# Small loads issued ahead of the opening barrier, and two split points moved, in a LoRA linear kernel

## The chip, the cores and the metric

One core of one Trainium2 chip. The time is the device time of one execution in microseconds (us), lower is better; it is quoted as the median of the runs, with lowest and highest. "Faster" and "slower" are verdicts at 2%. The span of a profile is about 1.3 us shorter than the time.

## The reference, cut to what matters

```python
x = randn(16, 2048, 256)            # fp32; W 256x256, A 256x16, B 16x256, E 16, scale 1.0
x_flat = x.reshape(-1, in_dim)      # 32768 x 256
y = x_flat @ W
lora_out = ((x_flat @ lora_A) * lora_E) @ lora_B
y = y + scale * lora_out            # 32768 x 256, fp32
```

33.6 MB are read and 33.6 MB are written, for one small matrix product. The kernel folds A, E and B into one matrix, weff = W + A diag(E) B, once at its start.

## The kernel before: the parts that the change and the argument touch

The 32768 rows are 4 chunks of 64 rows per partition (8.4 MB each). The kernel keeps three chunks at a time in SBUF, the on-chip memory, in three "homes"; chunk 3 uses the home of chunk 0 again, so its loads wait until the rows of chunk 0 that they overwrite have been stored. Results are written over x in its home. All loads and stores of rows are issued by one engine, SP, in the order of one list:

```python
ORDER = [
    ("L", 0, 0, 8),          # load, chunk, first row, end row
    ("W",),
    ("L", 0, 8, 24), ("L", 0, 24, 40), ("L", 0, 40, 64),
    ("L", 1, 0, 32), ("L", 1, 32, 64),
    ("L", 2, 0, 16), ("L", 2, 16, 64),
    ("S", 0, 0, 44),         # store
    ("S", 0, 44, 64),
    ("L", 3, 0, 44),
    ("L", 3, 44, 64),
    ("S", 1, 0, 64), ("S", 2, 0, 64), ("S", 3, 0, 64),
]
HELD = (2, 16)                   # from this row on the cast waits for the store in HOLDERS
HOLDERS = (("S", 0, 0, 44),)
...
    def sync_program():
        for n, op in enumerate(ORDER):
            ...
            if kind == "L":
                for st in stored:            # stores of the rows that this load overwrites
                    if st[1] == c - N_HOMES and st[2] < e and s < st[3]:
                        sync.wait_ge(stored[st], 16)
                ins = sync.dma_start(out=at_home, in_=x_chunks[c, :, s:e, :]).then_inc(loaded[op], 16)
                if n == 0:
                    opening.append(ins.ins.name)     # issued ahead of the opening barrier
            else:
                sync.wait_ge(s_done, ends.index((c * ROWS + e) // CG - 1) + 1)
                sync.dma_start(out=y_chunks[c, :, s:e, :], in_=at_home).then_inc(...)
```

A group of 4 rows passes through four engines: POOL casts it to bf16 (line 176 of this kernel), PE transposes it (226), DVE copies the transpose to SBUF (210), PE multiplies by weff (237), ACT copies the result into the home (193). The setup needs A, E, B and W, in this order. Everything named in `opening` is moved ahead of the barrier that all engines pass at the start; before the change, these are the first rows of x and A. The final wait of SP for the last stores is line 268. PE is the matrix engine; DVE, ACT and POOL are the vector, scalar and general-purpose engines; SP issues transfers. The 16 DMA engines, which move the data, are meant where the text below speaks of "the engines" of a queue or of "one engine" that is slow.

## Time and profile before

161.79 us when the prediction was made (median of 3, 161.79 to 162.03).

| what | value | where read |
|---|---|---|
| span | 160.5 us | page |
| main DMA queue, share of 16 engines | 98.3% | page, part 3 |
| bytes over the span | 420 GB/s | page, part 3 |
| busiest compute engine (PE) | 61% | page, part 1 |
| end of compute of chunk 3 | 121.97 us | timeline of ACT |
| SP waits for the last stores | 36.7 us | waits of SP |

These lines are from the page of the kernel before: span; PE, POOL, granted clock of PE (PEclk, tenths of full speed) and DMA share in 40 slices of 4 us (the other digits are tenths of busy time); the main queue with packets, MB, share; the bytes.

```profile
span 160.5 us, 2023 instructions
...
PE   5999999959999991000899948999991000000000
...
POOL 1526758477777740001677716777720000000000
PEclk9999999999999999755599995999999555555555
DMA  7999999999999998999999899997997997997991
...
q1 hardware_dynamic: 2304, 67.37, 98.3%
...
HBM read 33.85 MB, written 33.55 MB: 420 GB/s over the span
...
```

DMA is at 9 in nearly every slice (the 7s and 8s further on come from long packets that are counted where they start; in the packet records no engine idles there), while PE and POOL have a long hole (slices 15 to 18, counted from 0, where the cast of chunk 2 is held) and nothing at all in the last quarter.

The chain of waits of the kernel before seems to say something else. The columns are start, duration in us, and what:

```profile
...
2.48 20.82 DMA home<-in_x_dram
...
28.46 47.02 DMA out_dram<-home
...
75.50 20.25 DMA home<-in_x_dram
...
120.96 1.01 ACT home L193
```

The store issued at 28.46 us takes 47.02 us "to land", and the chain then follows compute of chunk 3. But this is a place in a queue, not a slow store: all loads of chunks 0 to 2 are ahead of it. The view of SP's timeline (start, time over which the group is issued, instruction) shows how early the issues are, and the waits of SP (total us, times, longest) show how long SP waits for the last stores when all is issued:

```profile
...
0.00 0.38 SPq L147 DMA_DIRECT2D home<-in_x_dram  x1
1.14 0.33 SPq L139 DMA_DIRECT2D w_sb<-in_W_dram  x1
1.52 3.54 SPq L147 DMA_DIRECT2D home<-in_x_dram  x7
28.46 8.76 SPq L152 DMA_DIRECT2D out_dram<-home  x2
75.50 7.19 SPq L147 DMA_DIRECT2D home<-in_x_dram  x2
82.73 39.63 SPq L152 DMA_DIRECT2D out_dram<-home  x3
```

```profile
...
SPq L268 <- SPq L268: 36.7, 1, 36.7
...
```

Seven loads of x, 24 MB, are in the queue by 5.1 us. The start of the kernel before, in the timeline of all engines:

```profile
...
1.10 0.38 ACTq L187 DMA_DIRECT2D e_sb<-in_lora_E_dram  x1
...
1.15 0.20 POOL L155 MEMSET ident<- 128x128 f32 x1 [0.71 <-SPq L272]
1.51 0.45 ACTq L187 DMA_DIRECT2D b_sb<-in_lora_B_dram  x1
...
7.47 2.07 PE L259 MATMUL psum_y<-b_sb,ate 16*128 16x256 f32 x4 [0.30 <-DMA b_sb<-in_lora_B_dram]
...
9.64 0.69 DVE L214 TENSOR_TENSOR weff<-w_sb,psum_y 128x512 bf16<-128x512 f32 x1 [1.75 <-PE psum_y L259]
...
```

The barrier is passed at about 1.1 us; the identity is made (1.15), E and B are issued (1.10, 1.51), the product with B runs at 7.47 and weff is made at 9.64 us.

Beside these views the argument uses the trace's records of single DMA packets (start, duration, bytes), which no view prints; tables of them stand in plain fences. One packet is one partition's share of a load or store, so 8 packets per engine and transfer. At full rate a 64 KB packet takes 2.418 us, 48 KB 1.816, 44 KB 1.665, 32 KB 1.215, 24 KB 0.912, 20 KB 0.761: 16 engines at 2.418 us per 64 KB are 433.7 GB/s.

### The profile page before, as it was taken

The numbers are of one execution on the slowest core, as the hardware profiler recorded it, in microseconds if no ns is written. First come the engines' busy times: TensorE is split into PE (matmuls) and PEld (weight loads), VectorE is DVE, ScalarE is ACT, GpSimd is POOL, SyncE is SP. The second block draws the span as 40 slices with busy tenths as digits, with TensorE's granted clock in tenths as the row PEclk, the third lists the DMA queues.
The fourth block names the chain that finished last, engine by engine and source line by source line (L and its number), as shares of the span: only waits on it lengthen the run. The fifth ranks groups of instructions, "written<-read, shape, count | busy, mean of one in ns | idle before, by whom it ended". The sixth has DMA issues, their size and how long they took to land.

```text
span 160.5 us, 2023 instructions
## 1 busy us (share of the span) xinstructions
PE 97.5 (61%) x782; PEld 84.3 (53%) x782; DVE 45.4 (28%) x66; ACT 66.1 (41%) x65; POOL 66.8 (42%) x70
## 2 busy tenths in 40 slices
PE   5999999959999991000899948999991000000000
PEld 2358988949999990000799937999990000000000
DVE  0233554525555550000255521555540000000000
ACT  3005776737777773000177751777773000000000
POOL 1526758477777740001677716777720000000000
PEclk9999999999999999755599995999999555555555
DMA  7999999999999998999999899997997997997991
GB/s 251 398 441 455 416 463 392 474 433 400 416 445 502 453 404 359 505 393 394 421 402 496 382 404 451 500 492 310 506 457 343 490 474 343 490 474 343 490 457 82
DMA packets 2515, 67.43 MB, mean 420 GB/s; under 512 B 448, under 2 KB 464, under 8 KB 592
## 3 DMA queue, kind: packets, MB, share of 16 engines
q1 hardware_dynamic: 2304, 67.37, 98.3%
q10 hardware_dynamic: 208, 0.03, 0.1%
q14 instruction: 3, 0.02, 0.0%
HBM read 33.85 MB, written 33.55 MB: 420 GB/s over the span
## 4 chain that ended last, share of the span: by engine, by line
DMA 55%; PE 17%; POOL 1%; ACT 1%; SPq 1%; issue 1%; ACTq 0%
DMA out_dram<-home 29%; DMA home<-in_x_dram 26%; PE psum_y L237 11%; PE psum_xt L226 6%; POOL stage L176 1%; ACT home L193 1%; SPq L147 1%; SPq L139 0%; ACTq L195 0%; SPq L308 0%; SPq L272 0%
## 5 line engine op out<-in xcount | busy, mean ns | idle before, releaser
L193 ACT COPY home<-psum_y 128x1024 f32<-128x1024 f32 x64 | 64.8, 1013 | 53.9 <-PE psum_y L237 53.9
L176 POOL CAST stage<-home 128x1024 bf16<-128x1024 f32 x64 | 66.1, 1040 | 49.2 <-DMA out_dram<-home 17.3
L237 PE MATMUL psum_y<-weff,xt 128*128 128x256 bf16 x512 | 69.7, 281 | 0.0
L210 DVE COPY xt<-psum_xt 128x1024 bf16<-128x1024 bf16 x64 | 44.3, 692 | 66.0 <-PE psum_xt L226 66.0
L237 PEld LDWEIGHTS psum_y<-weff,xt 128*128 128x128 bf16 x512 | 51.8, 101 | 6.5
L226 PE MATMUL psum_xt<-ident,stage 128*128 128x128 f32 x260 | 42.1, 286 | 21.2 <-POOL stage L176 21.2
L226 PEld LDWEIGHTS psum_xt<-ident,stage 128*128 128x128 f32 x260 | 32.0, 148 | 24.6 <-issue 23.4
L250 PE MATMUL psum_y<-ident 128*128 128x512 f32 x4 | 3.8, 1101 | 1.9 <-POOL ident L157 1.9
L250 PEld LDWEIGHTS psum_y<-ident 128*128 128x128 f32 x4 | 1.2, 325 | 3.0 <-POOL ident L157 1.9
L259 PE MATMUL psum_y<-b_sb,ate 16*128 16x256 f32 x4 | 2.1, 670 | 0.3 <-DMA b_sb<-in_lora_B_dram 0.3
L200 DVE TENSOR_SCALAR ate<-psum_y,e_sb 16x256 f32<-16x256 f32 x1 | 0.5, 472 | 6.3 <-PE psum_y L253 6.3
L193 ACT ACT_TABLE_LOAD x1 | 1.3, 1283 | 2.0 <-issue 2.0
L259 PEld LDWEIGHTS psum_y<-b_sb,ate 16*128 16x128 f32 x4 | 1.2, 319 | 0.9 <-DMA b_sb<-in_lora_B_dram 0.7
L214 DVE TENSOR_TENSOR weff<-w_sb,psum_y 128x512 bf16<-128x512 f32 x1 | 0.7, 689 | 1.8 <-PE psum_y L259 1.8
L253 PEld LDWEIGHTS psum_y<-ident,a_sb 128*16 128x16 f32 x2 | 0.2, 114 | 1.3 <-DMA a_sb<-in_lora_A_dram 0.9
L253 PE MATMUL psum_y<-ident,a_sb 128*16 128x128 f32 x2 | 0.6, 421 | 0.0
L155 POOL MEMSET ident<- 128x128 f32 x1 | 0.2, 204 | 0.7 <-SPq L272 0.7
L157 POOL TENSOR_SCALAR_AFFINE_SELECT ident<-ident 128x128 f32<-128x128 f32 x1 | 0.3, 292 | 0.2 <-POOL ident L155 0.2
L294 POOL MEMSET const-float32-0.0<- 128x1 f32 x1 | 0.1, 99 | 0.2 <-issue 0.2
L294 POOL MEMSET const-bfloat16-1.0<- 128x1 bf16 x1 | 0.1, 102 | 0.0
L294 POOL MEMSET const-uint8-127<- 128x1 uint8 x1 | 0.1, 102 | 0.0
L294 POOL MEMSET const-float32-1.0<- 128x1 f32 x1 | 0.1, 99 | 0.0
## 6 DMA issues: line engine op xcount, KB each, us to landing
home<-in_x_dram SPq DMA_DIRECT2D x2, 4096.0 KB, 34.7
home<-in_x_dram SPq DMA_DIRECT2D x3, 2048.0 KB, 14.0
home<-in_x_dram SPq DMA_DIRECT2D x1, 6144.0 KB, 57.6
out_dram<-home SPq DMA_DIRECT2D x1, 5632.0 KB, 47.0
home<-in_x_dram SPq DMA_DIRECT2D x1, 5632.0 KB, 20.3
home<-in_x_dram SPq DMA_DIRECT2D x1, 3072.0 KB, 20.8
out_dram<-home SPq DMA_DIRECT2D x1, 2560.0 KB, 45.5
home<-in_x_dram SPq DMA_DIRECT2D x1, 2560.0 KB, 19.5
```

The source lines that it names most:

```text
L147: ins = sync.dma_start(out=at_home, in_=x_chunks[c, :, s:e, :]).then_inc(loaded[op], 16)
L176: gpsimd.tensor_copy(out=stage[g % NS][:], in_=home(c)[:, b:b + CG, :]).then_inc(s_stage[g % UNROLL], 1)
L193: scalar.copy(out=home(c)[:, b:b + CG, :], in_=psum_y[g % NY][:]).then_inc(s_free[(g + NY) % UNROLL], 1)
L200: vector.tensor_scalar(out=ate[:], in0=psum_y[0][:R, :KT, :P], scalar1=e_sb[:], scalar2=float(scale), op0=ALU.mult, op1=ALU.mult,).then_in ...
L210: vector.tensor_copy(out=xt[g % NX][:], in_=psum_xt[g % NT][:].bitcast(BF16)).then_inc(s_xt[g % UNROLL], 1)
L214: vector.tensor_add(out=weff[:], in0=w_sb[:], in1=psum_y[1][:, :KT, :]).then_inc(s_free[0], 1)
L226: ins = tensor.transpose(psum_xt[i % NT][:, b, :], words[:, b, :], ident[:])
L237: ins = tensor.matmul(psum_y[i % NY][:, b, :], xt[i % NX][:, b, t::KT], weff[:, t, :], start=(t == 0), stop=(t == KT - 1),)
L250: tensor.matmul(psum_y[1][:, :2, :], ident[:], ident[:, None, :].to_broadcast([P, 4, P]), start=True, stop=True)
L253: ins = tensor.transpose(psum_y[0][:R, t, :P], a_sb[:, t, :], ident[:])
L259: ins = tensor.matmul(psum_y[1][:, t, :], ate[:, t, :], b_sb[:], start=True, stop=True)
L294: nc = _bacc.Bacc("TRN2", target_bir_lowering=False, num_devices=1)
```

## The change

The intent: take the setup's small loads off the path behind the barrier, so that weff is made earlier, and choose the split points so that the cast of chunk 2 and the compute of chunk 3 start earlier.

```diff
-    ("S", 0, 0, 44),
-    ("S", 0, 44, 64),
-    ("L", 3, 0, 44),
-    ("L", 3, 44, 64),
+    ("S", 0, 0, 40),
+    ("S", 0, 40, 64),
+    ("L", 3, 0, 32),
+    ("L", 3, 32, 64),
...
-HOLDERS = (("S", 0, 0, 44),)
+HOLDERS = (("S", 0, 0, 40),)
...                                    # in sync_program, the load of W
-                sync.dma_start(out=w_sb[:], in_=w).then_inc(set_up_loaded["w"], 16)
+                ins = sync.dma_start(out=w_sb[:], in_=w).then_inc(set_up_loaded["w"], 16)
+                opening.append(ins.ins.name)
...                                    # in scalar_program, the loads of A, B, E
             ("a", a_sb, lora_A.rearrange("(q t) r -> q t r", t=KT)),
+            ("b", b_sb, lora_B),
             ("e", e_sb, lora_E[:, None]),
-            ("b", b_sb, lora_B),
...
-            if name == "a":
-                opening.append(ins.ins.name)
+            opening.append(ins.ins.name)
```

The order of the instructions on each engine is otherwise the same; SP's load of W and ACT's loads of B and E move ahead of the barrier.

## The prediction

> **What bounds the kernel now.** The 16 DMA engines, from end to end. The page gives the main queue a share of 98.3% and a mean of 420 GB/s. In the trace's packet records all 16 engines are occupied from about 1.2 us (first packet 1.03) to 158.1 us of a 160.5 us span; the only holes, between 3 and 6 us, are worth 0.1 us of all engines. A 64 KB packet takes 2.418 us, so 16 engines give 433.7 GB/s. This agrees with the ceiling of 435 GB/s in the Trainium skill, "DMA: Bandwidth & Descriptors", section "Where 436 GB/s comes from". 67.37 MB at that rate are 155.3 us. The rest is 1 us of start, some 2 us of longer packets at load/store turns, and a tail: 15 engines end between 158.1 and 159.3 us, one at 160.0. That one lost 1.4 us: its 64 KB packets took 2.57 instead of 2.42 us from 100.6 to 123.7 us, while chunk 3 was computed (until 122.0).
>
> The chain of waits names a load (20.8 us), a store (47.0 us) and chunk 3's matmuls, but the queue is first-in-first-out: the store issued at 28.5 lands at 75.5 us because all earlier loads are ahead of it. Compute has slack: the stores reach chunk 3 at about 139 us, 17 us after its rows are done.
>
> **What the change does.**
> - W, A, B, E ahead of the barrier: moves four issues of 0.33 to 0.45 us. The order of the queue and the bytes stay. The first 1 MB keeps the engines busy until about 4.3 us, and the next load, issued at 1.52 us, was early enough. Three issues on ScalarE (0.12 + 0.38 + 0.45 + 0.39, ending near 1.3 us instead of 0.5) will delay the barrier by an estimated 0.4 to 0.8 us; the second load of x is issued at 1.6 to 2.0 us. Nothing starves. B lands before its wait (today 7.4 us; 0.7 us waited), but the second load of x, landing near 11 us, gates compute anyway. Worth 0 +- 0.1 us. The same page, "Issuing engines are not separate DMA queues", says that issuing elsewhere saves only sequencer time; I expect agreement.
> - Store 0 split at 40: lands about 1.2 us earlier (0.5 MB less), near 74.3 us; the held cast of chunk 2 starts then. Off the critical path.
> - Chunk 3 in halves: the first lands near 91.2 us instead of 95.8; compute ends near 116 to 118 instead of 122.0 us. Off the critical path; packets of 40, 24, 32 KB instead of 44 and 20 cost the same (estimate from the records: +0.04 us).
> - Indirect: if the one engine's slow packets come from compute beside the store of chunk 1, ending compute 5 us earlier spares it two of nine, 0.3 us of the end.
>
> **Prediction.** 161.5 us, range 160.9 to 162.1. Faster by over 2%: 0.01; within 2%: 0.98; slower: 0.01.
>
> **What would show it.** Loads of x up to chunk 2 and the last three stores land within 0.2 and 0.5 us of before; mean 419 to 422 GB/s; in the timeline W is issued before 1 us, the second load of x at 1.6 to 2.0; the first store within 1 us of 28.5; compute of chunk 3 ends 4 to 6 us earlier without moving the end.
>
> **What would make it wrong.** A hole in the queue: a chunk-3 load issued after the queue drained (today 6 to 7 us of remaining store cover it); a barrier so late that engines idle at 4 us; or another engine lagging, up to 1 us either way.

## The result, and the profile after

| kernel | median us | lowest to highest | runs | ratio to before, 95% interval |
|---|---|---|---|---|
| before | 161.71 | 161.61 to 162.03 | 6 | |
| after | 161.59 | 161.40 to 161.92 | 6 | 0.9993 (0.9976 to 1.0009) |
| after, repeated in later rounds | 161.32 | 161.20 to 162.46 | 6 | 0.9990 (0.9960 to 1.0020) |

If there is a gain, it is 0.1%, and neither interval excludes none. The same lines of the page after:

```profile
span 160.4 us, 2024 instructions
...
PE   2969978959999991000899999999930000000000
...
POOL 1527838477777740001657777787300000000000
PEclk9999999999999999655579999999995555555555
DMA  7999999999999997989999999997998998998992
...
q1 hardware_dynamic: 2304, 67.37, 98.5%
...
HBM read 33.85 MB, written 33.55 MB: 420 GB/s over the span
...
```

The DMA row is again at 7 to 9 in every slice but the last, and the 420 GB/s are the same; PE and POOL end a slice earlier (the last PE digit that is not 0 moves from slice 30 to 29). Chain, timeline of SP, wait for the last stores, and start:

```profile
...
2.95 20.34 DMA home<-in_x_dram
...
27.14 48.41 DMA out_dram<-home
...
75.66 1.05 POOL stage L177
...
```

```profile
...
0.43 0.42 SPq L139 DMA_DIRECT2D w_sb<-in_W_dram  x1
2.10 3.39 SPq L148 DMA_DIRECT2D home<-in_x_dram  x7
27.14 10.06 SPq L153 DMA_DIRECT2D out_dram<-home  x2
75.56 7.74 SPq L148 DMA_DIRECT2D home<-in_x_dram  x2
83.35 35.85 SPq L153 DMA_DIRECT2D out_dram<-home  x3
```

```profile
...
SPq L268 <- SPq L268: 39.7, 1, 39.7
...
```

```profile
...
0.55 0.45 ACTq L188 DMA_DIRECT2D b_sb<-in_lora_B_dram  x1
1.02 0.44 ACTq L188 DMA_DIRECT2D e_sb<-in_lora_E_dram  x1
...
2.10 0.20 POOL L156 MEMSET ident<- 128x128 f32 x1 [1.66 <-SPq L272]
...
7.83 1.10 PE L259 MATMUL psum_y<-b_sb,ate 16*128 16x256 f32 x4
...
9.03 0.69 DVE L214 TENSOR_TENSOR weff<-w_sb,psum_y 128x512 bf16<-128x512 f32 x1 [0.58 <-PE psum_y L259]
...
```

Everything that the change meant to move has moved. W is issued at 0.43 instead of 1.14 us, B at 0.55 instead of 1.51, weff is made at 9.03 instead of 9.64, store 0 is issued at 27.14 instead of 28.46, compute of chunk 3 ends at 118.80 instead of 121.97 (timeline of ACT). And there is a price: the barrier is passed 0.95 us later (the identity at 2.10 instead of 1.15), because ACT issues until 1.46 us. The chain of waits has another shape (it now goes through the cast of chunk 2 at 75.66), yet the time is the same. Of the 3.2 us that compute gained, 3.0 reappear in one place: SP's wait for the last stores grew from 36.7 to 39.7 us.

One more thing changed. POOL's timeline, first of the kernel before, then of the one after, and the last result of chunk 3 in the one after:

```profile
...
95.81 2.02 POOL L176 CAST stage<-home 128x1024 bf16<-128x1024 f32 x2 [4.16 <-DMA home<-in_x_dram]
...
```

```profile
...
93.44 1.04 POOL L177 CAST stage<-home 128x1024 bf16<-128x1024 f32 x1 [0.34 <-PE psum_xt L226]
...
117.79 1.01 ACT L193 COPY home<-psum_y 128x1024 f32<-128x1024 f32 x1 [0.30 <-PE psum_y L237]
...
```

Before the change, the cast of chunk 3 waits 4.16 us for the first part of its load. After it, POOL waits for no load of chunk 3: from the held cast at 75.66 us on, it waits for PE alone. So the end of compute is now set by when that cast starts and by the pace of compute, not by the load of chunk 3.

The landings, first to last of the 16 engines, from the trace's landing records (us from the start of the span):

```
transfer              before             after              after, repeated
load 2, rows 16-64    61.61 to 62.16     61.95 to 63.37     61.72 to 62.72
store 0, first part   74.95 to 75.48     74.07 to 75.55     73.83 to 74.84
load 3, first part    94.51 to 95.75     91.08 to 92.56     90.79 to 92.09
load 3, second part  100.61 to 101.84   100.79 to 102.37   100.50 to 101.80
store 1              119.92 to 121.67   120.10 to 121.75   119.81 to 121.23
store 3              158.51 to 160.48   158.71 to 160.38   158.41 to 159.87
```

The first two split parts land elsewhere, since they are smaller; once the queue has passed them, the second part of load 3 and all stores land where they did, within the spread of the engines. The span is the last number of the last line.

### The profile page after: what moved, and what is told of

It reads as the page before. It is cut to its first block, busy times and chain, and to the rows that moved or that the text cites. A ratio compares the mean times of both kernels' runs of the same rounds, so it can differ in the third digit from the quotient of the medians.

```text
span 160.4 us, 2024 instructions
## 1 busy us (share of the span) xinstructions
PE 93.6 (58%) x782; PEld 82.7 (52%) x782; DVE 45.4 (28%) x66; ACT 66.1 (41%) x65; POOL 66.9 (42%) x70
## 4 chain that ended last, share of the span: by engine, by line
DMA 43%; PE 26%; POOL 1%; ACT 1%; SPq 0%; issue 0%; ACTq 0%; POOLq 0%
DMA out_dram<-home 30%; PE psum_y L237 17%; DMA home<-in_x_dram 13%; PE psum_xt L226 9%; POOL stage L177 1%; ACT home L193 1%; SPq L148 0%; ACTq L195 0%; SPq L308 0%; POOLq L176 0%; SPq L272 0%
## 5 line engine op out<-in xcount | busy, mean ns | idle before, releaser
L237 PE MATMUL psum_y<-weff,xt 128*128 128x256 bf16 x512 | 68.1, 277 | 0.0
L237 PEld LDWEIGHTS psum_y<-weff,xt 128*128 128x128 bf16 x512 | 51.0, 100 | 5.8
L226 PE MATMUL psum_xt<-ident,stage 128*128 128x128 f32 x260 | 40.7, 280 | 21.1 <-POOL stage L177 20.8
L259 PE MATMUL psum_y<-b_sb,ate 16*128 16x256 f32 x4 | 1.1, 393 | 0.1
L259 PEld LDWEIGHTS psum_y<-b_sb,ate 16*128 16x128 f32 x4 | 0.7, 184 | 0.4 <-issue 0.3
```

What stands on the lines that cost most here:

```text
L226: ins = tensor.transpose(psum_xt[i % NT][:, b, :], words[:, b, :], ident[:])
L237: ins = tensor.matmul(psum_y[i % NY][:, b, :], xt[i % NX][:, b, t::KT], weff[:, t, :], start=(t == 0), stop=(t == KT - 1),)
L259: ins = tensor.matmul(psum_y[1][:, t, :], ate[:, t, :], b_sb[:], start=True, stop=True)
```

## The experiments

The theory, Q: the DMA queue is full from about 1.2 us to the end, so only bytes, the rate of the packets and holes in the queue count; issue times, setup and compute are slack. The rivals: the start counts (S); the chain of waits is right and compute of chunk 3 is on the critical path (C). A second theory, B, concerns the last 1 to 2 us: one engine that ends last was slowed by compute that runs beside a store.

### The two halves of the change, one at a time

The first kernel has the small loads ahead of the barrier and the old ORDER and HOLDERS; the second has the new ORDER and HOLDERS and the old issues.

```diff
 # e1_ahead_only: the change without this
-    ("S", 0, 0, 40), ("S", 0, 40, 64), ("L", 3, 0, 32), ("L", 3, 32, 64),
+    ("S", 0, 0, 44), ("S", 0, 44, 64), ("L", 3, 0, 44), ("L", 3, 44, 64),
-HOLDERS = (("S", 0, 0, 40),)
+HOLDERS = (("S", 0, 0, 44),)
```

> Only W, A, B, E ahead of the barrier; stores and loads split as before. Theory Q (the DMA queue is full from end to end, everything else is slack): 161.6 +- 0.3 us, ratio 0.998 to 1.001; second load of x issued at 2.1 us instead of 1.5, W at 0.4, compute of chunk 3 ends near 122 as before. Rival S (the start matters: the earlier B and W are worth something at the end): ratio 0.996 or lower, the end moves by the 0.5 us by which weff is made earlier.

> Only store 0 split at row 40 and chunk 3 in halves. Theory Q: within 0.3 us of before (161.4 to 161.9); compute of chunk 3 ends near 119 instead of 122 us, last landing unmoved but for the one engine with slow packets, about 8 of them instead of 9. Rival C (the chain of waits is right, and compute of chunk 3 is on the critical path): 3 us faster, ratio 0.98.

Measured: e1_ahead_only 161.72 us (161.56 to 162.47), ratio 1.0007 (0.9986 to 1.0028). e2_split_only 161.52 us (161.11 to 162.48), ratio 0.9999 (0.9973 to 1.0025). Each half moves its own events and not the end. The timeline of SP, first of e1_ahead_only, then of e2_split_only:

```profile
...
0.43 0.43 SPq L139 DMA_DIRECT2D w_sb<-in_W_dram  x1
2.09 3.43 SPq L148 DMA_DIRECT2D home<-in_x_dram  x7
28.65 8.01 SPq L153 DMA_DIRECT2D out_dram<-home  x2
...
```

```profile
...
27.16 10.05 SPq L152 DMA_DIRECT2D out_dram<-home  x2
...
```

So the earlier issue of store 0 (27.16) comes from its split, which needs one group less, not from the earlier weights (28.65 in e1_ahead_only, even 0.2 us later than before). Compute of chunk 3 ends at 122.51 us in e1_ahead_only and at 117.03 in e2_split_only (119 had been expected): 5.5 us apart, and 0.2 us in the medians. Theory Q stands; S (0.996 or lower for the first) lies below its interval, and C (0.98 for the second) is excluded.

### Is compute slack? The hold moved to the end

```diff
 # e4_hold_moved: against the changed kernel
+            if (c, b) == (3, 32):
+                gpsimd.wait_ge(stored[("S", 1, 0, 64)], 16)   # this store gets a semaphore of its own
```

> The changed kernel with the second half of chunk 3 held until store 1 has landed (about 121.7 us), so its 8 groups are computed beside store 2 (about 122 to 133 us), not beside store 1. Theory B: slow packets of one engine from 100 to about 105 us, none until 121, then about 4 or 5 from 122 to 133; the sum of its excess stays near 1.0 to 1.2 us; the time is unchanged although compute of chunk 3 ends some 14 us later. Rival H: slow packets remain at 100 to 121 us and none in store 2. Rival C (compute of chunk 3 is critical): 14 us slower.

Measured: 161.40 us (161.32 to 162.26), ratio 0.9989 (0.9967 to 1.0011). From its page (PE, POOL and the granted clock in slices of 4 us), and from its waits (us in total, times, longest):

```profile
...
PE   2979969959999990000999999900003999100000
...
POOL 1537838387777730003577597300005472000000
PEclk9999999999999997555699999975555699955555
...
```

```profile
...
POOL stage L179 <- DMA out_dram<-home: 36.7, 2, 19.8
...
```

Compute now stops in slices 26 to 29 and ends at 137.77 us, 19 us later than in the changed kernel, and the time is not longer. Compute of chunk 3 has at least these 19 us of slack; C is excluded. (I had said 14 us later. One reason for the rest is that the half chunk met the granted clock at 5 tenths when it began, in slice 30; the whole difference was not taken apart.)

### What counts: bytes and holes

Two kernels take bytes away and put a hole in. The first leaves out the store of the last 8 rows per partition (its result is wrong, those rows stay unwritten); the second issues the second load of x only when the first rows have landed.

```diff
 # e5_less_stored
-    ("S", 3, 0, 64),
+    ("S", 3, 0, 56),
 # e6_late_load
+                if n == 2:
+                    sync.wait_ge(loaded[ORDER[0]], 16)
                 ins = sync.dma_start(out=at_home, in_=x_chunks[c, :, s:e, :]).then_inc(loaded[op], 16)
```

> The changed kernel without the store of the last 8 rows of chunk 3 (1.05 MB; the result is wrong on purpose, rows left unwritten). Everything is computed as before. Theory Q (full DMA queue): 1.05 MB at 433.7 GB/s = 2.4 us faster, 159.1 +- 0.3. Rival C (the chain of waits, compute or latency bound): 0 to 0.5 us.

> The changed kernel with the second load of x issued only when the first rows have landed (about 4.9 us instead of 2.1). Theory Q: the engines run dry at about 4.9 us (first rows and W done) and get the next packet about 1 us after the issue, so a hole of 0.8 to 1.3 us, all later landings of x and the end shifted by it: 162.6 +- 0.4. This shows what margin the issue at 2.1 us has. Rival S0 (issue times of the start do not reach the end at all, because later slack takes them up): 161.6.

Measured: e5_less_stored 159.17 us (158.71 to 159.67) against 161.63 of before in the same rounds: 2.46 us less, ratio 0.9837 (0.9804 to 0.9869), for 1.05 MB that take 2.42 us at 433.7 GB/s. A byte costs its full time. e6_late_load 162.99 us (162.86 to 163.19), ratio 1.0084 (1.0066 to 1.0101), 1.4 us slower than the changed kernel. Its timeline of SP:

```profile
...
4.82 3.32 SPq L150 DMA_DIRECT2D home<-in_x_dram  x7
...
```

The packet records show the hole: between 5 and 6 us only 2.2 of the 16 engines are occupied, and the holes between 3 and 7.5 us are worth 1.05 us of all engines (0.10 in the changed kernel). The first packet of the late load comes at 5.78 us, 0.96 us after the issue. The hole explains 0.95 of the 1.4 us. Most of the rest is that the packets of the late load itself took longer than usual, by 0.71 us per engine against 0.26 in the changed kernel. So an issue that comes too late does reach the end, undiminished; and the changed kernel's issue at 2.10 us is early enough, by an estimated 1.6 us: the engines take up its first packets at about 4.7 us, less 0.96 us. This is why neither the 0.6 us by which the second load comes later, nor the 0.7 us by which W comes earlier, can be seen.

### The danger that the split must avoid

If store 0 is split at 40 but the load of chunk 3 still at 44, the first load overwrites rows of both parts of the store.

```diff
 # e10_crossed: against the changed kernel
-    ("L", 3, 0, 32), ("L", 3, 32, 64),
+    ("L", 3, 0, 44), ("L", 3, 44, 64),
```

> The changed kernel with the loads of chunk 3 split at row 44 as before, but store 0 at row 40, so the first load of chunk 3 must wait for both parts of store 0 (rows 40 to 44 lie in the second). Theory Q: it is issued at about 82.4 us when the queue has just drained, and its first packet comes about 1 us later, so there is a hole of 1.2 to 1.8 us and the end is that much later: 163.0 +- 0.4. This is the hole that the prediction named as a danger and the change avoids. Rival (slack takes it up): 161.6.

Measured: 165.77 us (165.67 to 165.94), ratio 1.0246 (1.0219 to 1.0274), slower. Its timeline of SP, and its busy times in a stretch and, in the second of the two fences, in the same stretch of the changed kernel (the last two columns are the DMA share and GB/s):

```profile
...
82.60 0.81 SPq L148 DMA_DIRECT2D home<-in_x_dram  x2
...
```

```profile
...
81.00:84.00 3.00, 3.00 (x27) 2.66 (x25) 1.11 (x2) 1.87 (x2) 1.74 (x3) 0.91 0.65 206
...
```

```profile
...
81.00:84.00 3.00, 3.00 (x23) 2.65 (x22) 0.91 (x2) 1.28 (x2) 1.64 (x2) 0.76 1.17 505
...
```

The load is issued at 82.60 us instead of 75.56. The 16 engines had ended store 0 between 81.00 and 82.18 us and got the next packet between 83.57 and 84.36: a hole of about 2.5 us of all engines, not 1.2 to 1.8. I had forgotten that a landing is that of the slowest engine, and that all others idle until then. The rest, about 1.6 us, is packets that took longer than usual: 0.70 us per engine when the loads begin again (0.03 in the changed kernel), and 0.96 us in the 20 KB packets of the second load (97.6 to 105 us), which run into store 1. The direction was right and the size was off by a factor of nearly three (1.4 expected, 4.2 measured against the changed kernel's 161.59).

### The last engine

In the packet records of the kernel before, one engine takes 2.57 us for each 64 KB packet in a stretch of store 1, where all others take 2.418. It ends last. Theory B says that compute beside a store does this. Its rival, H, says that it belongs to the addresses of store 1. The kernel above with the moved hold tells them apart, and so does one without the hold, where chunk 2 is computed beside store 0:

```diff
 # e3_no_hold: against the changed kernel
-            if (c, b) == HELD:
-                for op in HOLDERS:
-                    gpsimd.wait_ge(stored[op], 16)
```

> The changed kernel without the wait that holds the cast of chunk 2 until store 0 has landed, so chunk 2 is computed beside store 0 (about 60 to 78 us). Theory B (a store that runs beside compute has one DMA engine with packets 6% slower; that engine then ends last): that engine's packets of store 0 are slow too, about +0.7 us more lag (7 packets of 40 KB at about +0.09), end 0.3 to 0.7 us later, about 162.1. Rival H (the slow packets belong to store 1's addresses, not to compute): store 0 clean, time unchanged at 161.6.

Packets of that one engine (records of packets, followed from end to start; times are us from the start of the span):

```
kernel                        compute beside stores      slow packets         lost by this engine
before                        101 to 122                 9, from 100.6 to 123.7   1.42 in stores 1 to 3
changed                       101 to 119                 8, from 100.4 to 120.9   1.24
moved hold (e4_hold_moved)    101 to 104, 122 to 138     none from 105 to 120,    1.11
                                                         again from 122 to 140
no hold (e3_no_hold)          63 to 82, 101 to 119       store 0 as well          1.19, and 0.83 in store 0
```

With the moved hold all packets that start between 105 and 120 us take 2.42 us, and the slow ones come back with compute, in store 2. Without the hold, one engine loses 0.37 and 0.46 us in the two parts of store 0 and 1.19 us more in store 1; the span is 161.1 us, and the time is 162.07 us (161.89 to 162.46), ratio 1.0018 (1.0002 to 1.0034). That is about 0.4 us over the changed kernel's ratio of the first rounds, though the two intervals overlap a little; it is what the hold in this kernel seems to be worth. H is excluded: the slow packets follow compute, not store 1. Beside loads there is next to nothing: from 82 to 100 us, with compute running, the same engine's 32 KB packets in the changed kernel took at most 0.01 us more than the usual 1.215. Three things stay open, and they keep B from being the whole story. It is not shown why it is one engine and which part of compute does it; something that merely goes along with running instructions, such as the writing of the profiler's own records, would show the same in these runs, and no run tests this. The slow packets go on for one packet after compute has ended (in the kernel before until 123.7 us, compute ended at 121.97); the trace of the next experiment says more on this. And beside the second part of store 0 in the changed kernel, where compute runs from 75.7 us on at half the granted clock, this engine's eight 24 KB packets show no excess (0.00 us); with the moved hold the packets at half clock show 0.06 and 0.08 us instead of 0.15. So the effect is weaker or absent at half clock; no run here tells whether the clock or the pace of compute sets it.

I tried to find out which engine it is. The statement of the Trainium skill that this rests on is in "DMA: Bandwidth & Descriptors", section "Why a DMA increments its semaphore by 16 and not by 1":

> The changed kernel with the last 4 rows of chunk 3 stored by 16 stores of 1, 2, ... 15 and 8 partitions, which go to the lowest-numbered engines if the Trainium skill is right on how the engines are chosen, so each engine's count of 4 KB packets (16 for engine 0 down to 0 for engine 15) tells which one it is. Theory F (it is a fixed engine that is slow beside compute): the chain with the slow packets has one count, here and in a later repeat; no guess for which. Time: the low-numbered engines get up to 16 instead of 8 packets of 4 KB, about 1.2 us more, so about 160.5 to 162.5 us, later if the slow one is low-numbered.

```diff
 # e7_marked: rows 60 to 64 of chunk 3
+                    for k in [*range(1, 16), 8]:
+                        part = slice(p, p + k)
+                        sync.dma_start(out=y_chunks[c, part, s:e, :], in_=at_home[part]).then_inc(stored_rest, 16)
+                        p += k
```

Measured: 164.04 us (163.32 to 164.30), outside the range that I had given. The attempt failed: the 4 KB packets of different engines lie within a few ns of each other, so for many of them more than one chain fits, and the counts can't be read. So no run here shows whether the skill is right on how the engines are chosen, and of the slow engine's number nothing follows; the tail got 2.4 us longer with these small uneven stores.

But the trace settles another point. SP's last issues, from its timeline:

```profile
...
118.10 13.82 SPq L158 DMA_DIRECT2D out_dram<-home  x16
```

Compute ends at 118.03 us here, and SP issues its last store only at 131.9. Followed through its packets, the slow engine is back at 2.42 to 2.43 us per 64 KB from 120.6 to 130.3 us, and then has two slow packets, from 130.25 to 135.27 us, of 2.47 and 2.55 us. No compute runs then. In the kernel before, in e1_ahead_only and with the moved hold, too, the last slow packets run while or just after SP ends its last issue (122.36, 122.90 and 138.16 us), which there comes 0.4 us after compute. So this tail, some 0.15 to 0.2 us in these profiles, seems to go with SP's last issue and not with compute; it is one trace that parts the two, and what happens at that moment is not shown.

### The turns of the queue

The packet records have a third term. Where the queue turns from loads to stores or back, packets take longer for a short while. The prediction put "some 2 us" on this; in the kernel before, the two turns of the table come to 0.66 us. Summed over the packets beyond the usual time for their size, divided by 16 engines (us):

```
kernel             turn to store 0   turn to load 3   sizes at the second turn
before                  0.26              0.40        20 KB, then 44 KB
e1_ahead_only           0.96              0.28        20 KB, then 44 KB
e2_split_only           0.60              0.03        24 KB, then 32 KB
changed                 1.01              0.03        24 KB, then 32 KB
changed, repeated       0.68              0.03        24 KB, then 32 KB
e3_no_hold              0.67              0.00        24 KB, then 32 KB
e4_hold_moved           0.98              0.03        24 KB, then 32 KB
e8_small_at_turn        0.55              0.03        24 KB, then 32 KB
```

The second turn is cheaper with the new split, in every profile: about 0.3 us per engine. The first turn is anything between 0.26 and 1.01 us, in kernels that do the same there. If the packets' sizes make the second turn cheap, smaller packets should make the first one cheap too:

```diff
 # e8_small_at_turn: against the changed kernel
-    ("L", 2, 16, 64), ("S", 0, 0, 40),
+    ("L", 2, 16, 40), ("L", 2, 40, 56), ("L", 2, 56, 64), ("S", 0, 0, 8), ("S", 0, 8, 40),
-HOLDERS = (("S", 0, 0, 40),)
+HOLDERS = (("S", 0, 0, 8), ("S", 0, 8, 40))
```

> The changed kernel with small packets where the queue turns from loads to store 0: rows 16 to 64 of chunk 2 loaded as 24, 16 and 8 rows instead of 48 at once, store 0 begun with 8 rows, then 32. Theory P (the loss at a turn grows with the packets that meet there: 44 and 20 KB cost 0.28 to 0.40 us per engine at the second turn, 24 and 32 KB 0.03): the excess at the first turn falls from 0.7 to 1.0 us to 0.3 or less, end 0.4 to 0.7 us earlier, about 161.1, which would beat both kernels by a little. Rival T (the turn costs a time of its own, whatever the packets): excess stays at 0.6 to 1.0, time 161.6.

> The changed kernel once more, beside the next two on the same chip, as their base. Theory Q: 161.6 +- 0.3 us, ratio to before within 0.997 to 1.001, one engine with about 8 packets of 2.57 us in store 1; the excess of packet time at the turn from loads to store 0 again 0.6 to 1.0 us per engine, at the turn from store 0 to the loads of chunk 3 at most 0.1.

Measured: e8_small_at_turn 161.42 us (160.98 to 162.10), ratio 0.9978 (0.9950 to 1.0005); the changed kernel in the same rounds 161.32 us, ratio 0.9990 (0.9960 to 1.0020). The excess at the first turn is 0.55 us, between what the two theories said, and within what this turn does anyway. So the size of the packets is not shown to be the cause, and this version is not shown to beat either kernel. The turn after these, from load 3 to store 1, speaks against the sizes too: in the kernel before and in e10_crossed it is the same, 20 KB packets, then 64 KB, and the 20 KB packets took 0.03 us per engine beyond the usual in the one and 0.96 us in the other. What makes the first turn vary, and whether it is the sizes or the instant that make the second one cheap, stays open; both are below 0.5% of the time.

## Why the prediction was right or wrong, point by point

- **161.5 us, 161.4 to 161.9 in six runs (median 161.59).** Right, and for the reason given: the queue is full, and the change moves neither bytes nor holes. The controls (bytes taken away, holes put in, compute put off by 19 us) each confirm a part of it. That the point lies within 0.1 us is in part luck: six runs span 0.5 us, and the turn to store 0 alone differs by up to 0.75 us between profiles.
- **"Nothing starves", worth 0 +- 0.1 us.** Right in the result (ratio 1.0007 for this half alone). The barrier came 0.95 us later, not 0.4 to 0.8, and the second load of x at 2.10 us, not 1.6 to 2.0. ACT's last issue ahead of the barrier ended at 0.51 us before and at 1.46 after (timeline), and this difference of 0.95 us went to the barrier in full; I had the end at 1.3 and took off more for no reason.
- **Store 0 lands near 74.3 us, 1.2 us earlier.** Its engines landed between 74.07 and 75.55 us; the cast began at 75.66, so nearly nothing was gained in this profile. In the repeat the last landing was 74.84. The step that failed is that the arrival at this point is that of before less 4 rows: the turn to store 0 cost 1.01 us per engine in this profile and 0.26 in that of before, and a landing is that of the slowest engine.
- **Compute of chunk 3 ends near 116 to 118 us, 4 to 6 us earlier.** 118.80 in the profile, 118.19 in the repeat, so 3.2 and 3.8 us earlier: the sign right, the size too large. The step that failed, as the prediction reads, is that it hung this end on the landing of the first part of load 3. The cast of chunk 3 no longer waited for that load; the end now hung on the held cast of chunk 2, which started at 75.66 us instead of the 74.3 forecast.
- **"Loads of x up to chunk 2 land within 0.2 us".** Right for all but the last of them, which landed at 63.37 instead of 62.16 us; the same turn.
- **The first store "within 1 us of 28.5".** Wrong by 0.3 us: 27.14. I had not counted that a store of 40 rows waits for 10 groups instead of 11, which is one group, 1.3 us. The run with the split alone (27.16) and the one without it (28.65) show this.
- **"Packets of 40, 24, 32 KB instead of 44 and 20 cost the same" (+0.04 us).** At full rate yes; at the second turn they saved about 0.3 us per engine, which I had not foreseen. It is of the size of the noise at the first turn.
- **The indirect gain of 0.3 us from the slow engine.** That the slow packets go with compute was right, and shown by moving compute. Its size here: 8 slow packets instead of 9, 1.24 us lost instead of 1.42, so 0.2 us; and it does not carry over fully to the end, since two other engines ended at 160.02 and 160.03 us in the changed kernel while the slow one ended at 159.60.

Three statements of the Trainium skill were used here. "DMA: Bandwidth & Descriptors", section "Where 436 GB/s comes from", gives a ceiling of 435 GB/s; 433.7 GB/s within packets and 420 GB/s over the span agree. The same section says that between HBM and SBUF about 358 GB/s bind instead; in this program, which runs on one core, that limit did not bind (420 GB/s). The same page, section "Issuing engines are not separate DMA queues", says that issuing from several engines saves only time on the sequencer; no run here tests this, since the change moves no load to another engine, only ahead of the barrier on the same one (ratio 1.0007). What that section leaves to the reader is that issues ahead of a barrier can also delay the barrier, here by 0.95 us. That transfers of one queue are taken in order (same page, "Queues, rings and completion order": each DMA engine takes its descriptors in ring order) is what makes a store issued at 28.46 us land at 75.48.

## What to carry to other kernels

When the DMA row of the profile is full from end to end, ask of a change only whether it moves bytes, the rate, or a hole in the queue; times from issue to landing and the chain of waits then mostly measure a place in a queue. Test it with a control that must show an effect, such as a few rows less to store (here 2.46 us for 1.05 MB), before calling a null result understood. Moving a split point of a store needs the split of the load that overwrites it to be moved along, so that its wait ends while the queue still has work: here a mismatch of 4 rows cost 2.5%.

## What the Trainium skill lacked or had wrong

- "DMA: Bandwidth & Descriptors", section "Latency and other measured facts", gives about 600 ns to the first byte for transfers issued from SP or ACT. Here the first packet came 0.96 to 1.02 us after the start of the issue, three times (issue at 0.00, packet at 1.02; 4.82 and 5.78; 82.60 and 83.57). Part of this is the issue itself, 0.38 us in the timeline, so the two need not contradict each other; but for judging a margin it is the 1 us that counts.
- The same page does not say what a queue that runs dry costs: 1.4 us at the start, and 4.2 us in the middle, of which about 2.5 us were the hole and 1.6 us slower packets after it and at the next turn.
- No page that I found has a cost for the turn between loads and stores: 0.00 to 1.01 us per engine here.
- No page that I found says that compute beside a store slows one DMA engine: 2.57 instead of 2.418 us per 64 KB packet, in whichever store compute ran beside at full clock (6%), and in two packets around SP's last issue without compute (2.47 and 2.55 us). The page above calls engines 7 and 15 usually slower, by its best guess for another way of issuing; whether this is one of them could not be read.
- No page that I found has the price of issues ahead of a barrier: 0.39 to 0.45 us each on ACT, and the barrier later by 0.95 us for two more of them.
